# Split weights of the input projection, written to DRAM in the first segment and read back on GpSimd's queue in the second

## The chip, the cores and the metric

The kernel runs on one core of one Trainium2 chip. The metric is the device time of one execution in microseconds (us), the median over runs. The engines are named as in the profile: PE is TensorE (PEld its weight loads), DVE VectorE, ACT ScalarE, POOL GpSimd, SP SyncE, which here only issues transfers.

## The reference

One decoder layer of a hybrid model in f32, with 1024 tokens and 16 learned meta tokens ahead of them, model width 1024:

```
h = concat([meta, x])                                  # 1040 x 1024
h = h + 0.5 * swiglu(rmsnorm(h), ffn1)
u = rmsnorm(h)
aq, ak, av, az, abeta, aalpha, bcols, ga, gb = split(u @ w_in)
o_a = chunked_gated_deltanet(aq, ak, av, az, abeta, aalpha)   # 8 heads of 128
o_b = rwkv7(bcols)                                            # 16 heads of 64
h = h + (sigmoid(ga) * o_a + sigmoid(gb) * o_b) @ w_out
h = h + 0.5 * swiglu(rmsnorm(h), ffn2)
return rmsnorm(h)[:, 16:]
```

The change concerns `u @ w_in`. The result for a token depends on the earlier ones through the recurrences of the two branches, so the tokens are worked off in order.

## The kernel before

**Stages.** `ffn1`, then `middle` (projection, both recurrences, output projection), then `ffn2`. In `middle` the tokens are cut into two segments, of 528 (with the meta tokens) and of 512. Each segment runs through 8 iterations, one for each head of the DeltaNet branch and pair of heads of the RWKV branch; `schedule` (L167) writes out the order of the actions of all 16 iterations (strings at L184 to L189). One iteration projects its columns (`new_b`, `new_a`, `gates`), builds the small triangular systems of 64 and 128 tokens (`operands`), inverts them (`inverses`, `merge_blocks`), forms the transition terms (`transitions`) and runs the chain over the chunks (`chains`, `finish`). The inverses of one iteration are made while the chain of the one before runs. The actions are only written in this order: the scheduler that builds the program decides how the instructions of neighbouring actions are interleaved on each engine.

**The projection.** `w_in` is held as 75 tiles `win` of 128 x 1024 f32 (512 KB), each the weights of 128 columns. f32 products are made of three passes: weights and activations are split into a high part (rounded) and a low part (the rest), and `mm3` (L256) sums high x high, high x low and low x high over 8 blocks of 128 rows, 24 matmuls into one tile `pp` of PSUM. With 528 tokens each is cut in two. Both segments use all 75 tiles, so before the change each is loaded twice and split twice.

**How a tile comes.** `weight_order` (L192) lists all weight tiles in the order of use, `fetchw` (L217) fetches the next one, `loadw` (L229) hands out a tile and first fetches up to `AHEAD` = 1 tiles beyond it. A fetch is a transfer on SP's queue into `wraw` (2 buffers, L223), the high part on ScalarE (L159) and the low part on VectorE (L160), both into `w` (`WB` = 2 buffers of 1 MB). A raw buffer is free when both splits have read it, a split buffer when TensorE has done its matmuls. The weights of the output projection `wout` (L892, tiles `pwo`) take the same way.

**What else stands on these queues.** SP carries nearly all of the program's transfers, in program order per queue. In an iteration these are, beside the raw weights: the operands of the inverse to and from DRAM (`scr`, `scm`, then `Ub`, L1331 to L1342), the inverse's result (`scX`, `scY` written at L1369 and L1371, read as `Xc` at L1374 and as `Y` at L1378), `gp` (L1232), and the small gate weights `ugr` (L1561) and `upr` (L1074). The inverse itself is a chain of 31 pairs of VectorE instructions `tb` and `Xb` (L1364, L1366); its results are merged on TensorE by the tiles `iv` (L1399 to L1423), after GpSimd has copied a part of `Xc` into `XA` (L1380). `ugr` is split into `ug` by the same lines L159 and L160. In `transitions`, VectorE forms `mt` (L1472) and `AR` (L1475) from the tile `mp`, and TensorE forms `np` (L1056) after that. `gra` (L1252) is TensorE's first large product of `operands`, so from `gra` to `iv` TensorE has other work to do until the inverse is there: projection matmuls and the rest of the recurrence.

**The end.** The last two iterations have no new projections behind them. `fill` (L833) makes the output projection of the first segment there, as TensorE's work while the last inverse is made; the other one follows behind.

Of the kernel before, what the change touches and what calls it, by code (L numbers as in the profile page):

```python
# [8 lines left out]
F32 = mybir.dt.float32  # L9
F32R = mybir.dt.float32r  # L10
# [3 lines left out]
P = 128  # L14
D = 1024
KD = D // P
# [23 lines left out]
WB = 2  # L40
AHEAD = 1
S1 = 3
HK = KD // 2
# [63 lines left out]
def build(tc, nc, a):  # L107

    ctx = ExitStack()
    with ctx:  # L110
        g = K()
        g.tc, g.nc, g.a = tc, nc, a
        nc.scalar.preload_act_table_set("natural_log_exp_and_others")
        pad = ctx.enter_context(tc.tile_pool(name="pad", bufs=1, side="right"))
        nc.vector.memset(pad.tile([P, 24], F32, name="pad"), 0.0)
        const = ctx.enter_context(tc.tile_pool(name="const", bufs=1))
        wp = ctx.enter_context(tc.tile_pool(name="wp", bufs=2))
        dram = ctx.enter_context(tc.tile_pool(name="dram", bufs=1, space=bass.MemoryType.DRAM))
        g.mmctx = ctx.enter_context(ExitStack())
        main_banks(g, 2, 3, 8)  # L120
        g.const, g.wp, g.dram = const, wp, dram

        ones = const.tile([P, P], F32, name="ones")
        nc.gpsimd.dma_start(ones, a["ck"][:, :P])
        g.pk = const.tile([P, NPK], F32, name="pk")
        nc.gpsimd.dma_start(g.pk, a["pk"])

        def pv(n):
            o, w = PK[n]
            return g.pk[:, o : o + w]  # L130

        nc.vector.tensor_scalar(pv("omu"), pv("mu"), -1.0, 1.0, op0=ALU.mult, op1=ALU.add)
        nc.vector.tensor_scalar(pv("oka"), pv("ka"), -1.0, 1.0, op0=ALU.mult, op1=ALU.add)
        for n in ("w0", "a0"):
            nc.vector.tensor_scalar(pv(n), pv(n), -1.0, None, op0=ALU.mult)
        g.C = lambda n: ones if n == "ones" else g.ck[:, CK[n][0] - P : CK[n][0] - P + CK[n][1]]
        g.V = lambda n, i=0: g.pk[:, PK[n][0] + i : PK[n][0] + i + 1]

        hdr = [dram.tile([KD, P, sn], F32, name=f"hdr{s}") for s, (_, sn, _) in enumerate(SEGS)]
        mdr = [dram.tile([NJ, P, FULL], F32, name=f"mdr{s}") for s in range(2)]  # L140
        g.hdr, g.mdr = hdr, mdr
        g.sdr = dram.tile([NJ, P, P + CB], F32, name="sdr")
        g.gdr = [dram.tile([NJ, FULL], F32, name=f"gdr{s}") for s in range(2)]
        g.rdr = dram.tile([P, FULL], F32, name="rdr")
        g.h2dr = dram.tile([KD, P, FULL], F32, name="h2dr")
        g.h3dr = dram.tile([KD, P, FULL], F32, name="h3dr")
        g.hid = dram.tile([NF, P, T], F32, name="hid")

        g.worder, g.wready, g.wfetched, g.wused = list(weight_order()), [], 0, 0
        ffn1(g)  # L150
        middle(g)
        ffn2(g)


def split(g, src, hi, lo, eng=None, hi_eng=None):
    if hi_eng:
        hi_eng.tensor_copy(hi, src)
    else:
        g.nc.scalar.activation(hi, src, AF.Copy)  # L159
    (eng or g.nc.vector).tensor_tensor(lo, src, hi.bitcast(F32), op=ALU.subtract)  # L160
# [6 lines left out]
def schedule():  # L167

    last = 2 * NJ - 1
    yield "segment", 0  # L170
    for it in range(2):
        for act in FIRST[it].split():
            yield act, it
    for it in range(last + 1):
        order = {NJ - 2: BEFORE_SWITCH, NJ - 1: SWITCH, last - 1: LAST_BUT_ONE, last: FINAL}.get(it, REGULAR)
        for act in order.split():
            if act == "segment":
                yield act, 1
            else:
                yield act.rstrip("+"), it + act.count("+")  # L180
# [11 lines left out]
def weight_order():  # L192

    def down_order(n):
        f = 0
        for G in GROUPS:
            for _ in range(2 if f + G == NF else 1):
                for m in range(KD):
                    yield f"wdn{n}", (m, slice(None), slice(f, f + G)), G
            f += G  # L200

    def tiles(cts, j=0):
        for ct in cts:
            yield "win", (ct + j % NJ,), KD

    yield from down_order(1)
    for act, it in schedule():
        yield from tiles(USES.get(act, ()), 0 if act == "segment" else it)
    for _ in range(2):
        for m in range(KD):  # L210
            yield "wout", (m,), KD

    yield None
    yield from down_order(2)


def fetchw(g):  # L217
    if not g.worder[g.wfetched]:
        del g.worder[g.wfetched]
    name, idx, kk = g.worder[g.wfetched]  # L220
    g.wfetched += 1
    raw = g.wp.tile([P, KD, P], F32, name="wraw", tag="wraw", bufs=2)
    g.nc.sync.dma_start(raw[:, :kk, :], g.a[name][idx])  # L223
    w = g.wp.tile([P, 2, KD, P], F32R, name="w", tag="w", bufs=WB)
    split(g, raw[:, :kk, :], w[:, 0, :kk, :], w[:, 1, :kk, :])
    g.wready.append((name, idx, w))


def loadw(g, name, *idx):  # L229

    while g.wfetched < min(g.wused + 1 + AHEAD, len(g.worder)) and g.worder[g.wfetched]:
        fetchw(g)
    g.wused += 1
    n, i, w = g.wready.pop(0)
    assert (n, i) == (name, idx)
    return w


def main_banks(g, w, n, banks=6):

    g.mmctx.close()
    g.mmw = w
    pool = lambda name, bufs: g.mmctx.enter_context(
        g.tc.tile_pool(name=name, bufs=bufs, space=bass.MemoryType.PSUM, reuse_waits="tile"))
    g.mm = pool("mm", n)
    g.mx = pool("mx", banks - n * w)
# [19 lines left out]
class Rms:  # L266


    def __init__(self, g, sq, n, add_on=None):
        self.g, self.sq, self.n, self.acc, self.k = g, sq, n, None, 0  # L270
        self.eng = add_on or g.nc.vector
# [276 lines left out]
class Hidden:  # L548

    AHEAD = 3  # L550
# [18 lines left out]
    def ahead(self):  # L569
        for f in range(self.AHEAD):  # L570
            self.load(f)
        yield
        yield
        fetchw(self.g)
        yield
        yield
        self.first = self.put(self.tile(self.pool, F32R, "hd0", "hd0", 1, [2]))
        yield
        yield
# [312 lines left out]
def wout(g, mg, add):  # L892
    for m in range(KD):
        ho = add(m)
        w = loadw(g, "wout", m)
        ps = mm_tile(g, "pwo")
        mm3(g, ps, w, KD, lambda k: (mg[k][:, 0, :FULL], mg[k][:, 1, :FULL]))
        g.nc.vector.tensor_tensor(ho, ps, ho, op=ALU.add)
        yield m, ho
# [796 lines left out]
```

## Time and profile before

| what | value |
|---|---|
| median of three runs | 3086.55 us |
| lowest and highest | 3084.68 and 3089.25 us |
| the profiled execution | 3085.29 us |
| its span in the trace | 3083.5 us |
| TensorE busy | 96% of the span |
| VectorE, ScalarE, GpSimd busy | 64%, 45%, 12% |
| transfers | 287.19 MB, 93 GB/s on average |

How to read it: the profile is one execution, and its span is the time from the first to the last event of the trace; the execution's own time is 1.8 us longer. A row of waits names the waiting engine, the tile and the line, then the engine and the operation that ended the wait, then total us, number and longest. A row of the chain has start and length in us. A row of busy time by stage has the stage, its length, and for each engine the busy time with its count of instructions. In the trace, the first segment's iterations lie from about 800 us to 1474 us, 97 us each; the second segment's steady ones from 1777 us on, 88 us each.

### The profile page before, as it was taken

Reading aid. Unit: us, or ns where it says so; the run is one execution under the profiler, and the core shown is the slowest. Engines: PE = TensorE matmul, PEld = TensorE weight load, DVE = VectorE, ACT = ScalarE, POOL = GpSimd, SP = SyncE. Lnnn points to the kernel's source line nnn. Section 1 sums busy time; section 2 is a strip of 40 time slices with the busy share of each in tenths; the row PEclk is TensorE's granted clock in tenths of the full one; section 3 lists DMA queues with packets and bytes.
Section 4 is the critical chain, followed back from the end, with each engine's and each line's share of the span. In section 5 each row is a group of like instructions: output and inputs, shape, how many; then the busy total and the mean of one; then the engine's idle time right before and its main releaser. Section 6 shows DMA issues by size and latency. Waiting matters only on the chain.

```text
span 3083.5 us, 61656 instructions
## 1 busy us (share of the span) xinstructions
PE 2959.3 (96%) x25498; PEld 2539.0 (82%) x25498; DVE 1976.2 (64%) x3840; ACT 1376.7 (45%) x2404; POOL 354.9 (12%) x519
## 2 busy tenths in 40 slices
PE   8999999999899999999999999999999999999998
PEld 8999998998778888788777777777777888887886
DVE  6455454346677777787867877777866655555335
ACT  5322222126555656566566655665644432222114
POOL 0222220000001000001001000010100022222000
PEclk9999999999899999999999999999999999999999
DMA  3232224234222322333332332223354232224223
GB/s 125 82 97 83 83 86 158 79 101 140 62 74 73 79 70 59 85 79 75 97 89 73 84 81 75 75 75 84 109 148 165 68 104 94 83 83 170 86 78 114
DMA packets 257593, 287.19 MB, mean 93 GB/s; under 512 B 169296, under 2 KB 175440, under 8 KB 257312
## 3 DMA queue, kind: packets, MB, share of 16 engines
q1 hardware_dynamic: 253072, 271.43, 29.4%
q0 software_dynamic: 2512, 8.65, 0.7%
q8 instruction: 201, 3.29, 0.4%
q10 hardware_dynamic: 1728, 3.16, 0.3%
q14 instruction: 80, 0.66, 0.1%
HBM read 232.70 MB, written 50.47 MB: 92 GB/s over the span
## 4 chain that ended last, share of the span: by engine, by line
PE 54%; DVE 11%; ACT 7%; issue 2%; DMA 2%; SPq 0%; DVEq 0%; POOL 0%; ACTq 0%
PE pp L262 18%; PE pg L450 12%; PE pd L262 7%; PE pwo L262 3%; DVE w L160 1%; PE pg L474 1%; PE b L1542 1%; PE cs L1003 1%; PE gra L1252 1%; DMA ugr<-in_upg 1%; PE bkt L1281 1%; DVE tb L1364 1%; DVE mt L1472 1%; DVE Xb L1366 1%; PE vp L1056 1%
## 5 line engine op out<-in xcount | busy, mean ns | idle before, releaser
L262 PE MATMUL pp<-uk,w 128*128 128x512 f32 (+2 forms) x4824 | 975.1, 347 | 15.8 <-DVE w L160 9.3
L262 PEld LDWEIGHTS pp<-uk,w 128*128 128x128 f32 x4824 | 744.7, 191 | 109.1 <-DVE w L160 13.0
L159 ACT ACTIVATE w<-wraw 128x1024 fp32r<-128x1024 f32 (+2 forms) x330 | 326.3, 989 | 712.6 <-PE pd L262 287.6
L262 PE MATMUL pd<-hd,w 128*128 128x512 f32 (+2 forms) x2640 | 495.6, 349 | 11.3 <-DVE w L160 6.7
L262 PEld LDWEIGHTS pd<-hd,w 128*128 128x128 f32 x2640 | 427.5, 189 | 78.2 <-DVE w L160 8.6
L160 DVE TENSOR_TENSOR w<-wraw,w 128x1024 fp32r<-128x1024 f32 (+2 forms) x330 | 376.1, 1140 | 90.9 <-ACT w L159 85.7
L456 DVE TENSOR_TENSOR c<-c,pg 128x520 f32<-128x520 f32 (+1 forms) x280 | 189.2, 689 | 337.3 <-PE pg L450 278.3
L450 PE MATMUL pg<-bt,w 128*128 128x256 f32 (+2 forms) x2520 | 403.9, 317 | 0.0
L450 PEld LDWEIGHTS pg<-bt,w 128*128 128x128 f32 x2520 | 361.0, 188 | 32.9 <-DVE w L160 0.2
L450 PE MATMUL pg<-b,w 128*128 128x256 f32 (+2 forms) x2160 | 348.1, 317 | 0.2 <-DVE c L456 0.2
L450 PEld LDWEIGHTS pg<-b,w 128*128 128x128 f32 x2160 | 309.8, 188 | 28.5 <-PE pg L450 0.4
L419 POOL TENSOR_TENSOR wrx<-wrx 128x512 f32<-128x512 f32 x38 | 57.2, 1505 | 755.1 <-DVE w22b L160 515.3
L1364 DVE TENSOR_TENSOR tb<-Ub,Xb 115x126 f32<-115x126 f32 (+22 forms) x496 | 124.1, 250 | 11.0 <-DMA Ub<-scr 2.7
L1366 DVE TENSOR_TENSOR Xb<-Xb,tb 115x126 f32<-115x126 f32 (+22 forms) x496 | 125.3, 253 | 8.7
L159 ACT ACTIVATE w<-wrx 128x1024 fp32r<-128x1024 f32 (+1 forms) x64 | 58.1, 908 | 156.8 <-PE pg L450 152.3
L1173 DVE SCALAR_TENSOR_TENSOR acc<-xr,pk,acc 128x528 f32<-128x528 f32 (+1 forms) x144 | 109.0, 757 | 26.4 <-ACT acc L1169 25.3
L609 DVE SCALAR_TENSOR_TENSOR h<-pd,h 128x528 f32<-128x528 f32 (+1 forms) x64 | 44.6, 698 | 115.0 <-PE pd L262 115.0
L609 DVE SCALAR_TENSOR_TENSOR hh<-pd,hh 128x512 f32<-128x512 f32 x64 | 44.2, 690 | 109.7 <-PE pd L262 106.6
L262 PE MATMUL pwo<-uk,w 128*128 128x512 f32 x384 | 101.5, 414 | 4.2 <-DVE w L160 1.9
L262 PEld LDWEIGHTS pwo<-uk,w 128*128 128x128 f32 x384 | 73.6, 197 | 22.2 <-DVE w L160 2.7
L923 ACT ACTIVATE sh<-pp,pk 128x528 f32<-128x528 f32 (+1 forms) x54 | 37.5, 694 | 98.3 <-PE pp L262 98.3
L159 ACT ACTIVATE hd<-hr 128x1040 fp32r<-128x1040 f32 (+1 forms) x44 | 45.3, 1061 | 68.6 <-DMA hr<-hid 43.7
(397 smaller groups left out, 4143.1 us busy)
## 6 DMA issues: line engine op xcount, KB each, us to landing
wraw<-in_win SPq DMA_DIRECT2D x150, 512.0 KB
wraw<-in_wgu SPq DMA_DIRECT2D x44, 512.0 KB
wrx<-in_wgu SPq DMA_DIRECT2D x44, 512.0 KB
wraw<-in_wdn SPq DMA_DIRECT2D x48, 320.0 KB
wraw<-in_wdn SPq DMA_DIRECT2D x32, 384.0 KB
hid<-c SPq DMA_DIRECT2D x44, 260.0 KB
hr<-hid SPq DMA_DIRECT2D x22, 520.0 KB
hid<-c SPq DMA_DIRECT2D x44, 256.0 KB
```

The costliest lines, as they stand in the source:

```text
L159: g.nc.scalar.activation(hi, src, AF.Copy)
L160: (eng or g.nc.vector).tensor_tensor(lo, src, hi.bitcast(F32), op=ALU.subtract)
L262: g.nc.tensor.matmul(ps, lhsT=l, rhs=r, start=i == 0, stop=i == n - 1)
L419: sums.tensor_tensor(a22, a21, a22, op=ALU.add)
L450: nc.tensor.matmul(ps[:, c0 : c0 + cn], lhsT=l[:, x, k, :], rhs=r[:, k, y, c0 : c0 + cn], start=i == 0, stop=i == 3 * HK - 1)
L456: nc.vector.tensor_tensor(o, x, y, op=ALU.add)
L474: nc.tensor.matmul(ps[:, c0 : c0 + cn], lhsT=l[:, x, k, :], rhs=r[:, k, y, c0 : c0 + cn], start=i == 0, stop=i == 6 * HK - 1)
L609: nc.vector.scalar_tensor_tensor(hv, pd, 0.5, hv, op0=ALU.mult, op1=ALU.add)
L923: nc.scalar.activation(sh[:, 1 : 1 + n], ps, AF.Identity, scale=g.V("mu", i))
L1173: nc.vector.scalar_tensor_tensor(acc[:, :n], xr[:, tap : tap + n], V("convw", ct * 4 + tap), acc[:, :n], op0=ALU.mult, op1=ALU.add)
L1364: nc.vector.tensor_tensor(tv, U[:, i, i + 1 :].unsqueeze(2).to_broadcast([npt, nt, ncc]), X[:, i, 0:ncc].unsqueeze(1).to_broadcast([npt, n ...
L1366: nc.vector.tensor_tensor(X[:, i + 1 :, 0:ncc], X[:, i + 1 :, 0:ncc], tv, op=ALU.add)
```

## The change

In the first segment, each split tile of `win` is also written to DRAM as it is (both parts, 1 MB) by SP's queue. In the second segment `fetchw` loads no raw tile of `win` and splits none: `saved_tile` reads the split one back on GpSimd's queue. Two of three tiles come into a buffer of `w`; every third comes as two halves of 512 KB (k-blocks 0 to 3 and 4 to 7), into both buffers of `wraw`, and the class `Halves` hands `mm3` the block of the right half. So three tiles can be held at once, and `loadw` fetches one tile further ahead in the second segment. The output projection's tiles still come raw, through `wraw`.

```
@@ before ffn1(g)
+        g.wsp = dram.tile([75, P, 2, KD, P], F32, name="wsp")
+        g.wsaved = {}
+        g.wsecond = next(i for i, x in enumerate(g.worder) if x and x in g.worder[:i] and x[0] == "win")
@@ fetchw
-    raw = g.wp.tile([P, KD, P], F32, name="wraw", tag="wraw", bufs=2)
-    g.nc.sync.dma_start(raw[:, :kk, :], g.a[name][idx])
-    w = g.wp.tile([P, 2, KD, P], F32R, name="w", tag="w", bufs=WB)
-    split(g, raw[:, :kk, :], w[:, 0, :kk, :], w[:, 1, :kk, :])
+    if name == "win" and idx[0] in g.wsaved:
+        w = saved_tile(g, idx[0])
+    else:
+        raw = g.wp.tile([P, KD, P], F32, name="wraw", tag="wraw", bufs=2)
+        g.nc.sync.dma_start(raw[:, :kk, :], g.a[name][idx])
+        w = g.wp.tile([P, 2, KD, P], F32R, name="w", tag="w", bufs=WB)
+        split(g, raw[:, :kk, :], w[:, 0, :kk, :], w[:, 1, :kk, :])
+        if name == "win":
+            g.nc.sync.dma_start(g.wsp[idx[0]], w.bitcast(F32))
+            g.wsaved[idx[0]] = len(g.wsaved)
     g.wready.append((name, idx, w))
+class Halves:
+    def __init__(self, *ts):
+        self.ts = ts
+    def __getitem__(self, i):
+        p, x, k, m = i
+        return self.ts[k // HK][p, x, k % HK, m]
+def saved_tile(g, ct):
+    if g.wsaved[ct] % 3 < 2:
+        w = g.wp.tile([P, 2, KD, P], F32R, name="w", tag="w", bufs=WB)
+        g.nc.gpsimd.dma_start(w, g.wsp[ct].bitcast(F32R))
+        return w
+    ts = []
+    for k in range(2):
+        t = g.wp.tile([P, 2, HK, P], F32R, name="wh", tag="wraw", bufs=2)
+        g.nc.gpsimd.dma_start(t, g.wsp[ct][:, :, k * HK : (k + 1) * HK, :].bitcast(F32R))
+        ts.append(t)
+    return Halves(*ts)
 def loadw(g, name, *idx):
-    while g.wfetched < min(g.wused + 1 + AHEAD, len(g.worder)) and g.worder[g.wfetched]:
+    ahead = AHEAD + (name == "win" and idx[0] in g.wsaved and g.wused >= g.wsecond)
+    while g.wfetched < min(g.wused + 1 + ahead, len(g.worder)) and g.worder[g.wfetched]:
         fetchw(g)
```

In the program VectorE and ScalarE have 75 instructions fewer, GpSimd has 100 more (50 tiles `w`, 25 tiles of two halves `wh`), and SP as many as before (75 stores for 75 raw loads). Since the scheduler sets the order anew, other instructions move too. Lines of the kernel after stand 36 higher from `mm3` on.

VectorE in the first segment, an iteration's start before (`mt` and `AR` are the transition terms, `ug` and `upz` the small gate weights, `LT` the operands of the next inverse):

```order
L160 TENSOR_TENSOR w<-wraw,w 128x1024
L160 TENSOR_TENSOR ug<-ugr,ug 128x128
L1566 TENSOR_TENSOR ug<-ugr,ug 32x128
L1078 TENSOR_TENSOR upz<-upr,upz 64x128 x2
L1472 TENSOR_TENSOR mt<-mp,ck 64x4x64 x4
L1475 TENSOR_TENSOR AR<-mp,AR 128x4x64 x2
L1214 TENSOR_TENSOR LT<-grb,ck 128x4x128 x2
```

and after:

```order
L1508 TENSOR_TENSOR mt<-mp,ck 64x4x64 x2
L1511 TENSOR_TENSOR AR<-mp,AR 128x4x64
L1514 TENSOR_TENSOR vbk<-np,vbk 128x4x64
L1517 TENSOR_TENSOR yb<-np,yb 128x4x64
L1276 TENSOR_TENSOR kts<-gp,tk 128x4
L1514 TENSOR_TENSOR vbk<-np,vbk 128x4x64
L1517 TENSOR_TENSOR yb<-np,yb 128x4x64
L1515 TENSOR_TENSOR vbk<-vbk,gam 128x512
L1250 TENSOR_TENSOR LT<-grb,ck 128x4x128 x2
L1536 COPY rhm<-bm_14575 16x128
L164 TENSOR_TENSOR ug<-ugr,ug 128x128
L1602 TENSOR_TENSOR ug<-ugr,ug 32x128
```

The splits of `ug` stood directly ahead of `mt` and `AR`; now they stand behind them, and behind the sums with `np`.

SP in the first segment, from the inverse's result to the gate weights, before:

```order
L1369 DMA scX<-Xb 1536x1x16 x2
L1371 DMA scY<-Yt 816x1x32 x2
L1374 DMA Xc<-scX 128x12x32
L223 DMA wraw<-in_win 128x1024
L1378 DMA Y_7138<-scY 32x12x32 x4
L1384 DMA ym<-scY 16x2x16
L1385 DMA ym<-scY 16x16
L223 DMA wraw<-in_win 128x1024 x2
L1232 DMA gp<-gdr_88 128x512
L223 DMA wraw<-in_win 128x1024 x2
L1561 DMA ugr<-in_upg 128x256
```

and after:

```order
L1410 DMA Xc<-scX 128x12x32
L234 DMA wsp<-w 128x2048
L1414 DMA Y_7141<-scY 32x12x32 x4
L1420 DMA ym<-scY 16x2x16
L1421 DMA ym<-scY 16x16
L230 DMA wraw<-in_win 128x1024 x2
L234 DMA wsp<-w 128x2048
L230 DMA wraw<-in_win 128x1024
L234 DMA wsp<-w 128x2048
L230 DMA wraw<-in_win 128x1024
L234 DMA wsp<-w 128x2048
L1268 DMA gp<-gdr_88 128x512
```

A store `wsp` of 1 MB now stands between `Xc` and `Y`, where a raw load stood, and three more ahead of `gp`.

TensorE in the last iteration, before (`pp` is the projection, `gat` the gate, `pwo` the output projection, `iv` the first merge of the last inverse):

```order
L262 MATMUL pp<-uk,w 128x512 x11
L1003 MATMUL cs<-hl,bdr 128x512
L262 MATMUL pp<-uk,w 128x512 x7
L1003 MATMUL cs<-hl,bdr 128x512
L262 MATMUL pp<-uk,w 128x512 x43
L1581 MATMUL gat<-gds,ug 128x512 x3
L1581 MATMUL gat<-g_17736,ug 128x512
L262 MATMUL pwo<-uk,w 128x512 x85
L1399 MATMUL iv_26390<-Xc,LT 32x32 x16
L1399 MATMUL iv_26390<-Xc,UA 32x32 x8
```

and after:

```order
L298 MATMUL pp<-uk,w 128x512 x29
L298 MATMUL pp<-uk,wh 128x512 x24
L1617 MATMUL gat<-gds,ug 128x512 x3
L1617 MATMUL gat<-g_17804,ug 128x512
L1435 MATMUL iv_26296<-Xc,LT 32x32 x16
L1435 MATMUL iv_26296<-Xc,UA 32x32 x8
L298 MATMUL pwo<-uk,w 128x512
```

The 85 matmuls of the output projection that stood ahead of `iv` now stand behind it.

## The prediction

> **What bounds the kernel now.** I read the page first, then busy time by stage, then the waits of TensorE, then the chain of two iterations, and last the rows of the operations that the change touches. The page:
>
> ```profile
> span 3083.5 us, 61656 instructions
> PE 2959.3 (96%) x25498; PEld 2539.0 (82%) x25498; DVE 1976.2 (64%) x3840; ACT 1376.7 (45%) x2404; POOL 354.9 (12%) x519
> wraw<-in_win SPq DMA_DIRECT2D x150, 512.0 KB
> ```
>
> TensorE is busy for 2959.3 of 3083.5 us, and the change leaves its work alone (the same matmuls in another order). So what can be won is a part of 3083.5 - 2959.3 = 124.2 us of idle time, over the whole program; the splits and loads that go matter only where TensorE waits. By stage, the second column of numbers is the length, the third TensorE's busy time, and the last two the DMA share and GB/s: six iterations of the first segment, the switch between the segments, five iterations of the second segment, and the end of the recurrences:
>
> ```profile
> 893.00:1474.00 581.00, 554.31 (x6792) 474.86 (x6794) 440.42 (x1072) 341.13 (x697) 47.52 (x139) 1.00 0.28 74
> 1474.00:1777.00 303.00, 282.82 (x2962) 222.88 (x2964) 236.76 (x545) 181.94 (x345) 26.02 (x53) 0.98 0.32 85
> 1777.00:2216.00 439.00, 423.44 (x4625) 338.08 (x4621) 349.61 (x815) 263.59 (x501) 38.23 (x80) 1.00 0.30 80
> 2216.00:2400.00 184.00, 175.52 (x1473) 137.43 (x1470) 117.55 (x239) 79.22 (x142) 1.46 (x3) 0.97 0.49 157
> ```
>
> TensorE idles 581.00 - 554.31 = 26.7 us, then 20.2, 15.6 and 8.5 us. These four numbers bound what each stage can give back. What TensorE waited for in the first segment (first row), at the switch (next two) and in the steady second segment (last three), with total, times and longest:
>
> ```profile
> PE np L1056 <- DVE AR L1475: 6.4, 6, 2.3
> PE pp L262 <- DVE gg L1582: 3.4, 1, 3.4
> PE pp L262 <- DVE w L160: 3.4, 2, 2.8
> PE np L1056 <- DVE AR L1475: 4.7, 5, 2.0
> PE xp L1056 <- ACT at L1460: 2.7, 5, 1.0
> PE pp L262 <- DVE w L160: 0.6, 2, 0.4
> ```
>
> The wait for split weights itself is small: 0.6 us in five iterations of the second segment. A gain there comes mainly from VectorE and ScalarE being less busy when the recurrence needs them.
>
> **Part 1: the splits that go.** The rows of the raw tiles from the switch to the end:
>
> ```profile
> L159 ACT ACTIVATE w<-wraw x79: 1040/1052/1084, 1487.9 to 2258.7; 128x1024 fp32r<-128x1024 f32 x79
> L160 DVE TENSOR_TENSOR w<-wraw,w x79: 1206/1218/1310, 1489.0 to 2260.1; 128x1024 fp32r<-128x1024 f32 x79
> ```
>
> and VectorE's group in the five steady iterations alone:
>
> ```profile
> L160 DVE TENSOR_TENSOR w<-wraw,w 128x1024 fp32r<-128x1024 f32 x45 | 55.1, 1225 | 5.7 <-ACT w L159 5.6
> ```
>
> 75 of these 79 go (the others are the output projection's): 75 x 1.052 = 78.9 us of ScalarE and 75 x 1.218 = 91.4 us of VectorE. Nearly all of it lies beside TensorE's work. In the steady second segment the upper bound is the whole idle time, 15.6 us. I take 9: the 4.7 us of the np row (its chain through VectorE keeps the `ug` split ahead of it, but loses projection splits), the 2.7 us of the xp row in part and the 0.6, and about 2 us of shorter waits. Lower bound: the new loads wait behind other work on GpSimd and cost 8 us (third rival). At the switch the upper bound is 20.2 us; the two waits shown, 3.4 and 3.4 us, are on VectorE, which is busy for 236.76 of 303.00 us there and has some 25 splits less (the 79 without the 45 of the steady stretch and the handful of the end). I take 9, with bounds of 0 and 20.2.
>
> **Part 2: the read back.** Each tile is now 1 MB, where the raw one had 512 KB. The nearest loads on GpSimd's queue are 520 KB:
>
> ```profile
> L670 POOL DMA_DIRECT2D h<-in_hT x8: 527/530/557, 477.6 to 486.6; - x8
> DMA to landing us min/median/max: 5.1/8.5/15.1
> ```
>
> A 1 MB load should then take between 5.1 us (if the time is latency) and 2 x 8.5 = 17 us (if it is all transfer). I take about 9, near the median row, since eight loads shared the queue there. By the Trainium skill, "DMA: Bandwidth & Descriptors", section "Measured (HBM→SBUF, 128 partitions, SWDGE, issued from GpSimd)", a lone 1 MB load takes 6.15 us; by that the loads would be early with more to spare and the sum would not move. In TensorE's order a tile is asked for when the tile three before it is done, so two tiles of projection lie between. One matmul of 512 columns takes 9.77 / 43 = 0.227 us (row in part 4), a tile 24 x 0.227 = 5.5 us, two tiles 10.9 us: more than 9, less than 17. Recurrence work between them adds cover, so I cost this at nothing; without that cover 75 tiles could each show some of the 6 us. Each issue takes 0.53 us of GpSimd, 100 x 0.53 = 53 us of an engine that was busy 12%.
>
> A rule that speaks against the move: the waits of SP's queue,
>
> ```profile
> SPq L223 <- DVE w L160: 743.7, 156, 24.0
> ```
>
> are long (743.7 us over 156 waits), and moving loads off SP shortens what is queued behind them. The Trainium skill, the same page, section "Issuing engines are not separate DMA queues", says that all issuing engines share the same 16 DMA engines and that issuing from several saves only sequencer time. By that rule alone the move is worth nothing and costs the second half of each read; with DMA shares of 0.28 to 0.32 in the rows above there is room for it, and I keep the sum.
>
> **Part 3: the stores in the first segment.** 75 stores of 1 MB go on SP's queue, each ready when its split is. The chain of one iteration there, in order of time:
>
> ```profile
> 1181.05 3.47 DMA ugr<-in_upg
> 1187.83 0.43 DVE AR L1475
> 1188.40 1.33 PE np L1056 x56
> 1193.80 1.73 PE gra L1252 x8
> 1260.29 0.96 PE iv L1399 x48
> ```
>
> and SP's part that carries the inverse back:
>
> ```profile
> 1240.29 1.41 SPq L1369 DMA_DIRECT2D scX<-Xb  x2
> 1245.74 3.09 SPq L1374 DMA_DIRECT2D Xc<-scX  x1
> 1248.94 1.01 SPq L223 DMA_DIRECT2D wraw<-in_win  x1
> 1250.95 1.92 SPq L1378 DMA_DIRECT2D Y<-scY  x4
> ```
>
> Two things change. First, before, `AR` stood on VectorE behind the split of `ug`, whose raw tile landed late (3.47 us on the chain); after, the order puts `AR` ahead of it. The gain is at most the 6.4 us of the np row in the six iterations. I take 4. Second, between gra and iv the order had 315 projection matmuls in each of these iterations; after, it has 247 and 289 by turns. At 0.227 us per 512 columns (the tile of 528 columns is cut in two) that is 39.8 us before, and 35.0 and 39.2 after. Y's last issue ended at 1250.95 + 1.92 = 1252.87 and iv began at 1260.29, so landing and slack are 7.4 us together. After, cover is down by 4.8 us in every other iteration, and a 1 MB store stands directly ahead of Y on SP. Part 2 prices 1 MB at 9 us as a load; no store of that size is in the trace. If Y waits for none of it, the 4.8 us eat into the 7.4 and cost nothing; if Y waits for all of it, 4.8 + 9 - 7.4 = 6.4 us show in three of the six, and 9 - 7.4 = 1.6 in the others, 24 us in all. I take 2.3 us in each of three, 7 in all, nearer to nothing because stores and small transfers can run side by side at a DMA share of 0.28. Part 3 is -4 + 7 = +3 us, bounds -6.4 and +24.
>
> **Part 4: the end.** The last iteration's chain:
>
> ```profile
> 2225.43 1.92 PE gra L1252 x8
> 2253.84 9.77 PE pp L262 x43
> 2264.54 5.96 PE pwo L262 x26
> 2270.51 13.67 PE pwo L262 x59
> 2284.18 0.96 PE iv L1399 x48
> 2281.04 2.03 SPq L1378 DMA_DIRECT2D Y<-scY  x4
> ```
>
> Before, 26 + 59 = 85 matmuls of the output projection (19.6 us) covered the wait for the last inverse, and iv began just as Y was there (its last issue ended at 2283.07, iv began at 2284.18). After, the last projection tile comes as two halves in both raw slots, so the output projection's raw tiles can only be loaded when it is used up: order puts iv ahead of all of `pwo`, and 24 + 29 projection matmuls ahead. Counted between gra and iv, 179 projection matmuls become 112: 67 x 0.227 = 15.2 us less cover. VectorE's inverse loses four to seven splits of 1.218 us in that stretch (4.9 to 8.5 us), so TensorE would stand for 15.2 - 8.5 = 6.7 to 15.2 - 4.9 = 10.3 us. A part of it replaces the 8.5 us of idle time that were there. I take +7, with bounds +2 and +14.
>
> **Sum.** +3 - 9 - 9 + 7 = -8 us. The profiled execution took 3085.29 us (span 3083.5 and 1.8 around it), 1.3 under the median of the three runs, 3086.55; 3086.55 - 8 gives 3078.5. A change of 0.2%, 6 us, is about what a measurement of this kernel can tell from none. The lower bounds together (-6.4 - 20.2 - 15.6 + 2 = -40) and the upper ones (+24 + 0 + 8 + 14 = +46) are unlikely to meet.
>
> **Rivals.**
> - *Slower: the stores delay the recurrence.* Place: Y, `Ub` and `ugr` behind 1 MB stores on SP in the first segment. Price: the 24 us of part 3, plus some 4 for the seventh iteration of the segment; with the second segment's -18 and the end's +7 that is +17, or 3103.6. It decides from where a store delays Y by more than the 7.4 us less the 4.8. Against it: DMA share 0.28. For it: the small load of `ugr` already puts 3.47 us on the chain there. Chance 0.18.
> - *No change: the work that goes was beside TensorE.* The wait for split weights was 0.6 us in five iterations, so steady state and switch give some 10 together, and part 3 and 4 take them: 3086.5, within 6 us. Chance 0.22.
> - *Slower: GpSimd's queue is in order.* A tile's load stands behind the copy of XA, which waits for Xc. In the second segment that holds back the tile that follows iv. At 3 us in each of six iterations 18 us replace the steady gain of 9: 3086.5 + 3 - 9 + 18 + 7 = 3105.5, and 3096.5 where half of it shows. It decides where Xc lands later than the 10.9 us of two tiles ahead of the use. Chance 0.08.
> - *Slower: GpSimd's descriptor writes meet VectorE.* Each of the 100 issues would take longer beside VectorE's two-input work; the row above has 527 to 557 ns for eight issues, 30 ns apart, while VectorE worked. If each of 75 tiles came 0.3 us late, 22 us are lost: 3078.5 + 22 = 3100.5. Beside this stands the Trainium skill, "DMA: Bandwidth & Descriptors", section "SWDGE vs HWDGE vs iDMA", which says that these rings are written in SBUF under the lock that VectorE can hold. Chance 0.04.
> - *Much faster.* All of the idle time of switch and steady second segment goes (-20.2 - 15.6), and the rest stands at +3 + 7: -25.8, 3060.7. Chance 0.14.
> - That the change doesn't do what it says is ruled out by the order's counts: VectorE and ScalarE lose 75 rows each, GpSimd gains 100.
>
> **How the numbers follow.** The forecast of 3078.5 has 0.34; a tenth of that falls within 6 us of no change. Faster by over 0.2%: 0.31 + 0.14 = 0.45. Within: 0.22 + 0.03 = 0.25. Slower: 0.18 + 0.08 + 0.04 = 0.30. The range leaves out the ends: from 3058, somewhat under the much faster case, to 3105, where the slower cases end. The forecast's own range is 3066 to 3086. Both signs hold much of the chance.
>
> **What would show it.** In the profile after, by the same stages: no idle time of TensorE behind AR in the first segment, and the store's landing near 9 us; iv directly behind Y there would be the first rival. The switch and the five steady iterations should idle 9 us less each; a wait of `pp` for a DMA of `w` or `wh` is the third rival. At the end TensorE should stand some 7 us ahead of iv. Wrong I would be if the first segment is longer by over 10 us, or if the steady iterations keep their 15.6 us of idle time.

## The result, and the profile after

The changed kernel takes 3141.7 us (median of 4 runs, 3137.47 to 3145.62), the kernel before beside it 3087.9 us: a ratio of 1.0169 with a 95% interval of 1.0154 to 1.0184. It is slower by 1.7%, some 54 us, where 3078.5 was forecast with a range of 3058 to 3105. The page after:

```profile
span 3138.0 us, 61716 instructions
PE 3001.5 (96%) x25498; PEld 2578.4 (82%) x25498; DVE 1902.0 (61%) x3765; ACT 1314.6 (42%) x2329; POOL 392.8 (13%) x619
wsp<-w SPq DMA_DIRECT2D x75, 1024.0 KB
w<-wsp POOLq DMA_DIRECT2D x50, 1024.0 KB, 5.3
```

TensorE does the same 25498 matmuls, and is busy for 3001.5 us instead of 2959.3: 42 of the 54 us show as busy time. The splits are gone as counted (75 instructions fewer, their row on VectorE 376.1 to 284.0 us, VectorE as a whole 1976.2 to 1902.0). To see where the time lies I cut both programs at the same event, the first `np` of an iteration: five iterations of the first segment, the switch, six steady iterations of the second, and the rest. Busy time by stage before:

```profile
992.40:1477.60 485.20, 463.52 (x5629) 396.22 (x5630) 368.73 (x895) 282.59 (x574) 37.38 (x115) 1.00 0.29 76
1477.60:1700.30 222.70, 207.03 (x2129) 163.02 (x2130) 170.22 (x388) 131.24 (x246) 19.77 (x40) 0.98 0.31 82
1700.30:2223.00 522.70, 502.11 (x5548) 400.57 (x5549) 418.04 (x975) 317.28 (x605) 44.48 (x93) 1.00 0.31 83
2223.00:3083.50 860.50, 834.22 (x4220) 678.79 (x4220) 468.45 (x693) 273.88 (x390) 121.46 (x99) 0.99 0.33 108
```

and after:

```profile
999.90:1520.30 520.40, 486.65 (x5602) 418.76 (x5603) 372.41 (x896) 281.57 (x574) 29.80 (x115) 0.93 0.50 158
1520.30:1752.30 232.00, 215.10 (x2127) 170.02 (x2127) 151.12 (x370) 119.29 (x237) 34.58 (x65) 0.96 0.53 151
1752.30:2263.70 511.40, 500.67 (x5589) 399.32 (x5589) 363.26 (x926) 270.67 (x548) 78.78 (x166) 1.00 0.51 138
2263.70:3138.00 874.30, 842.29 (x4238) 685.65 (x4238) 467.47 (x692) 274.57 (x391) 122.21 (x102) 0.98 0.33 109
```

Length by stage: +7.5 us up to the first cut (992.4 to 999.9), then +35.2, +9.3, -11.3 and +13.8, together the 54.5 us by which the span grew. In the five iterations TensorE's busy time rose by 23.1 us and its idle time by 12.1, with the granted clock at 0.93 instead of 1.00. The third row holds the gain that was looked for: idle time fell from 20.6 to 10.7 us.

The first segment, in windows of 4 us around one `iv` after (behind the window and its length stands TensorE's busy time; the third number from the right is its granted clock):

```profile
1272.00:1276.00 4.00, 2.41 (x60) 2.09 (x58) 4.00 (x9) 2.74 (x5) 1.97 (x8) 1.00 1.07 325
1276.00:1280.00 4.00, 2.95 (x53) 2.01 (x54) 3.42 (x7) 0.97 (x2) 0.00 (x0) 0.62 0.48 113
1280.00:1284.00 4.00, 1.98 (x28) 1.69 (x22) 1.25 (x4) 2.49 (x5) 0.00 (x0) 0.50 0.43 174
1284.00:1288.00 4.00, 4.00 (x74) 3.67 (x73) 2.72 (x4) 2.33 (x5) 0.00 (x0) 0.60 0.01 4
```

and what TensorE did there, with the idle time ahead and its releaser in brackets:

```profile
1273.56 0.75 PE L1435 MATMUL iv<-Xc,LT 32*32 32x32 f32 x32 [0.17 <-DMA Xc<-scX]
1277.05 0.80 PE L1039 MATMUL bon<-hl,bdr 128*128 128x512 f32 x1 [2.46 <-ACT hl L163]
1282.02 1.08 PE L1454 MATMUL iv<-XA,UA 64*64 64x64 f32 x8 [1.55 <-DVE XA L1450]
1288.20 11.89 PE L298 MATMUL pp<-uk,w 128*128 128x272 f32 x96
```

`iv` began as soon as `Xc` was there. Between its stages stood no projection matmul, so TensorE waited for a column sum (`bon`) and for `XA`, and from the end of the first of these two gaps on the clock stood at half for some 10 us. Only then came 96 projection matmuls in one piece. The waits of the five iterations:

```profile
PE cs L1039 <- ACT hl L1053: 8.1, 5, 3.7
PE bon L1039 <- ACT hl L163: 7.8, 5, 2.5
PE np L1092 <- DVE AR L1511: 7.0, 5, 2.7
PE iv L1454 <- DVE XA L1450: 4.6, 3, 1.6
```

The chain before has the next `gra` 30 us behind `iv` (1260.29, and the row below); after, 46 us:

```profile
1290.50 1.73 PE gra L1252 x8
```

```profile
1214.62 1.73 PE gra L1288 x8
1273.56 1.05 PE iv L1435 x48
...
1319.48 1.73 PE gra L1288 x8
```

From `gra` to `iv` it is 58.9 us after instead of 66.5, so the inverse is ready sooner for the recurrence, and what was gained there is lost behind it.

That is the order of every other iteration. In those between, 289 projection matmuls stand ahead of `iv`, 48 between its stages and 10 from there to `np` (before: 315, 30 and 8), and they take as long: 104.4 us from `gra` to `gra` around the `iv` at 1383.61, against 104.9 in the one shown. Here TensorE waited for the column sums `cs` with nothing ahead of them, and the 48 came behind; before, 16 projection matmuls stood at that place. After, then before:

```profile
1390.85 0.81 PE L1039 MATMUL cs<-hl,onesr 128*128 128x256 f32 x2 [3.67 <-ACT hl L1053]
1394.12 6.31 PE L298 MATMUL pp<-uk,w 128*128 128x272 f32 x28
```

```profile
1264.66 3.93 PE L262 MATMUL pp<-uk,w 128*128 128x512 f32 x16
```

In both kinds of iteration the stretch from `gra` to `iv` is shorter than before, and the one from `iv` to the next `gra` is 8 to 16 us longer.

### The profile page after: what moved, and what is told of

Its sections match the earlier page's. It is cut to its first block, busy times and chain, and to the rows that moved or that the text cites. A ratio compares the mean times of both kernels' runs of the same rounds, so it can differ in the third digit from the quotient of the medians.

```text
span 3138.0 us, 61716 instructions
## 1 busy us (share of the span) xinstructions
PE 3001.5 (96%) x25498; PEld 2578.4 (82%) x25498; DVE 1902.0 (61%) x3765; ACT 1314.6 (42%) x2329; POOL 392.8 (13%) x619
## 4 chain that ended last, share of the span: by engine, by line
PE 81%; DVE 7%; ACT 5%; DMA 4%; issue 2%; SPq 1%; POOL 0%; DVEq 0%; ACTq 0%; POOLq 0%
PE pg L486 25%; PE pp L298 20%; PE pd L298 15%; PE pg L510 3%; PE pwo L298 3%; PE cs L1039 1%; PE xp L1092 1%; PE b L1578 1%; PE vp L1092 1%; PE gra L1288 1%; DMA Xc<-scX 1%; PE grb L1247 1%; PE bkt L1317 1%; PE mp L1092 1%; PE np L1092 1%
## 5 line engine op out<-in xcount | busy, mean ns | idle before, releaser
L298 PE MATMUL pp<-uk,w 128*128 128x512 f32 (+2 forms) x4224 | 823.3, 342 | 7.9 <-DMA w<-wsp 4.5
L298 PEld LDWEIGHTS pp<-uk,w 128*128 128x128 f32 x4224 | 641.7, 194 | 76.1 <-issue 11.3
L163 ACT ACTIVATE w<-wraw 128x1024 fp32r<-128x1024 f32 (+2 forms) x255 | 247.3, 970 | 694.7 <-PE pd L298 290.7
L298 PE MATMUL pd<-hd,w 128*128 128x512 f32 (+2 forms) x2640 | 496.3, 350 | 10.6 <-DVE w L164 6.5
L164 DVE TENSOR_TENSOR w<-wraw,w 128x1024 fp32r<-128x1024 f32 (+2 forms) x255 | 284.0, 1114 | 96.8 <-ACT w L163 92.3
L298 PE MATMUL pp<-uk,wh 128*128 128x512 f32 x600 | 161.1, 403 | 0.0
L298 PEld LDWEIGHTS pp<-uk,wh 128*128 128x128 f32 x600 | 109.0, 189 | 19.6
```

The costliest lines, as they stand in the source:

```text
L298: g.nc.tensor.matmul(ps, lhsT=l, rhs=r, start=i == 0, stop=i == n - 1)
```

## The experiments

Two theories stood against each other. **Theory A (order):** a store on SP's queue makes the scheduler place projection matmuls behind the inverse instead of beside it; TensorE runs dry around `iv`, its clock falls, and the iteration grows. **Theory B (traffic):** 75 MB of stores put off the transfers on the recurrence's path. Times below are medians, ratios against the kernel before beside them.

**e1, small stores on SP.**

```
-            g.nc.sync.dma_start(g.wsp[idx[0]], w.bitcast(F32))
+            g.nc.sync.dma_start(g.wsp[idx[0]][0:8], w[0:8].bitcast(F32))
...
```

> Edit: the change, but of each split tile only 8 of 128 partitions are stored (64 KB instead of 1 MB), and the read back takes 1 MB of the raw weights instead (the output is of other numbers). The order of the instructions on TensorE, VectorE and ScalarE is that of the change to the row. Theory A (order: the store on SP's queue makes the scheduler lay the projection matmuls elsewhere, TensorE runs dry around iv and np, and its granted clock drops there): the first segment stays as long as with the change, about 104 us an iteration, and the whole stays at 3135 to 3145 us. Theory B (traffic: 75 MB of stores delay the transfers of the inverse): nearly all of the 43 us of the first segment come back, 3095 to 3105 us.

3134.2 us, ratio 1.0142 (1.0127 to 1.0157). Without 15/16 of the bytes only 7.5 us came back. The five iterations still take 514.9 us at a clock of 0.95:

```profile
999.20:1514.10 514.90, 480.35 (x5603) 412.53 (x5604) 372.42 (x896) 281.00 (x574) 31.57 (x115) 0.95 0.30 75
```

Theory B alone falls for this order, and theory A came out as it said. The DMA share is back at 0.30, so the clock does not follow the traffic. The small store is still in the program here; what that leaves open is taken up with e9.

**e2, full stores on GpSimd's queue.**

```
-            g.nc.sync.dma_start(g.wsp[idx[0]], w.bitcast(F32))
+            g.nc.gpsimd.dma_start(g.wsp[idx[0]], w.bitcast(F32))
```

> Edit: the change with the stores issued on GpSimd's queue instead of SP's. All 75 MB are still stored; TensorE's order in the first segment is that of the kernel before (315 projection matmuls from gra to iv in each iteration). Theory A (order): the first segment goes back to 97 us an iteration within 1 us, the whole to 3095 to 3105 us. Theory B (traffic): the first segment stays at 102 us an iteration or more, the whole at 3130 to 3145 us.

3151.8 us, ratio 1.0195 (1.0176 to 1.0214): TensorE's order of before, and slower than the change. Theory A alone falls here. The chain over the length of an iteration has transfers on it:

```profile
1187.67 4.32 DMA wraw<-in_win
1217.14 8.29 DMA upr<-in_upwa
1240.04 7.47 DMA Ub<-scr
```

Before, the piece of that kind on the chain was `ugr` with 3.47 us, and no `Ub`. In the five iterations ScalarE waited longest for the raw tile that it splits:

```profile
ACT w L163 <- DMA wraw<-in_win: 28.8, 5, 6.0
```

**e3, the read back alone.**

```
-            g.nc.sync.dma_start(g.wsp[idx[0]], w.bitcast(F32))
-        g.nc.gpsimd.dma_start(w, g.wsp[ct].bitcast(F32R))
+        g.nc.gpsimd.dma_start(w, g.a["win"][min(ct, 73) : min(ct, 73) + 2].rearrange("t p k m -> p t k m").bitcast(F32R))
...
```

> Edit: no stores; in the second segment 1 MB of raw weights is read on GpSimd's queue for each tile as if it were the split one (the output is of other numbers). TensorE's order in the first segment is that of the kernel before. Both theories: the first segment as before, 97 us an iteration; steady second segment 86.5 us an iteration as with the change; the end longer by 14 us as with the change. Whole: 3085 to 3100 us. If the first segment is still slow here, both theories fall.

3092.7 us, ratio 1.0014 (1.0004 to 1.0023). The first segment has the order of before and in this trace ends 4.6 us later (1482.2 against 1477.6); the steady second segment gains as much as with the change, 511.1 us where before had 522.7:

```profile
1709.60:2220.70 511.10, 500.77 (x5589) 399.34 (x5590) 363.24 (x926) 270.63 (x548) 88.56 (x166) 1.00 0.52 138
```

But switch and end are longer by 4.7 (227.4 against 222.7) and 9.7 us (870.2 against 860.5), and the whole gains nothing.

**e4, the stores alone.**

```
-    if name == "win" and idx[0] in g.wsaved:
+    if False:
-    ahead = AHEAD + (name == "win" and idx[0] in g.wsaved and g.wused >= g.wsecond)
+    ahead = AHEAD
-        if name == "win":
+        if name == "win" and idx[0] not in g.wsaved:
```

> Edit: the stores alone; in the second segment the raw weights are loaded and split as before, nothing is read back. Both theories: the first segment as with the change (104 us an iteration, +43 us), the second and the end as before: 3125 to 3140 us. By theory A it equals the change in the first segment, since the order there is the same.

3140.6 us, ratio 1.0164 (1.0149 to 1.0179): the stores cost what the whole change costs.

**e5, small stores on GpSimd's queue.**

```
-            g.nc.gpsimd.dma_start(g.wsp[idx[0]], w.bitcast(F32))
+            g.nc.gpsimd.dma_start(g.wsp[idx[0]][0:8], w[0:8].bitcast(F32))
...
```

> Edit: the stores on GpSimd's queue (as in the run before with 1 MB each, 3151.8 us), but only 8 of 128 partitions of each tile (64 KB), and the read back takes raw weights (the output is of other numbers). The order on TensorE, VectorE and ScalarE is that run's to the row. Theory B (traffic): with TensorE's order of before, the 1 MB stores put off the landing of Ub and of the gate weights by 3 to 5 us each, 6 to 10 us an iteration; without the bytes the whole goes to 3092 to 3102 us. Theory C (GpSimd's queue: a store that waits for its split holds back the copies and memsets behind it): the whole stays above 3135 us.

3094.9 us, ratio 1.0022 (1.0012 to 1.0032). With the order of e2 to the row and without its bytes, 57 us are gone, so in this order the bytes cost them, and neither GpSimd's queue nor 75 waiting issues on it cost anything to speak of. ScalarE's wait for raw tiles is 2.7 us here. Which of the late transfers, raw tiles, `upr` or `Ub`, costs how much no run isolates. The landing of `Ub` in five iterations, first in e2:

```profile
DMA to landing us min/median/max: 7.3/7.4/7.5
```

then in e5:

```profile
DMA to landing us min/median/max: 4.1/4.4/4.6
```

**e6, the store issued when the tile is handed out.**

```
     g.wused += 1
     n, i, w = g.wready.pop(0)
+    if n == "win" and i[0] not in g.wsaved:
+        g.nc.sync.dma_start(g.wsp[i[0]], w.bitcast(F32))
+        g.wsaved[i[0]] = len(g.wsaved)
...
```

> Edit: the change with each store issued on SP's queue when the tile is handed out to TensorE, not when it is fetched. All 75 MB are stored. TensorE's order has 277 projection matmuls from gra to iv in the first segment and 66 between the merges of the inverse, where the change has 247 or 289, and 48 or 0. Theory A (order: TensorE runs dry around iv): most of the 30 us that the small stores still cost go, what is left is the traffic: 3105 to 3120 us. Theory B (traffic costs 6 to 10 us an iteration wherever the order leaves no slack): 3135 to 3150 us.

3124.3 us, ratio 1.0119 (1.0103 to 1.0135), between the two expectations: the place of a store in the program is worth 17 us, with the same bytes.

**e7, the last projection tile whole (on e3).**

```
-    if g.wsaved[ct] % 3 < 2:
+    if g.wsaved[ct] % 3 < 2 or ct == g.wlast:
...
```

> Edit: the read back alone (no stores, raw weights read; the output is of other numbers), and the last projection tile comes whole into a buffer of w, so that the raw buffers are free for the output projection. TensorE has 143 matmuls ahead of the last iv instead of 112 (31 x 0.227 = 7 us). Theory of the end (the halves in the raw buffers push the output projection behind the last inverse): 4 to 7 us under the read back alone at 3092.7, 3086 to 3089 us. Rival (the output projection is only moved, TensorE's wait there is not from it): within 2 us of 3092.7.

3090.8 us, ratio 1.0004 (0.9994 to 1.0014). That is 2 us under e3, at the rival's edge, and the intervals overlap so far that 4 us, the least that the theory expected, can't be ruled out: 7 us more of work ahead of `iv` gave some 2.

**e8, no further lookahead (on e3).**

```
-    ahead = AHEAD + (name == "win" and idx[0] in g.wsaved and g.wused >= g.wsecond)
+    ahead = AHEAD
```

> Edit: the read back alone (no stores, raw weights read; the output is of other numbers) without the further tile of lookahead. TensorE's order is the same as with it. If two tiles of lead cover the landing of 1 MB, as the prediction has it, one tile (5.5 us of matmuls and what stands between) does so only in part: 5 to 20 us slower than 3092.7. If the loads are early anyway: within 2 us of it.

3094.4 us, ratio 1.0020 (1.0011 to 1.0030): within 2 us. TensorE's order is the same with and without it, and the loads are early with either; in the steady second segment of the change the 1 MB loads land in

```profile
DMA to landing us min/median/max: 5.1/5.3/7.2
```

**e9, e6 with small stores.**

```
-        g.nc.sync.dma_start(g.wsp[i[0]], w.bitcast(F32))
+        g.nc.sync.dma_start(g.wsp[i[0]][0:8], w[0:8].bitcast(F32))
...
```

> Edit: as the run with each store issued when its tile is handed out (3124.3 us), on SP's queue, but only 8 of 128 partitions (64 KB), with the read back from raw weights (the output is of other numbers). TensorE's, VectorE's and ScalarE's order is that run's to the row. Theory A+B (two costs: the order of the fetch-time store leaves TensorE without work around iv, and the bytes delay the transfers of the recurrence): with this order and no bytes both are gone, 3090 to 3100 us. Rival D (a store on SP's queue, however small, holds back what is queued behind it until its split is there): above 3115 us.

3121.1 us, ratio 1.0113 (1.0098 to 1.0129): the bytes are some 3 us of e6's 35, within the intervals, and the two theories together had expected 3090 to 3100. That spoke for rival D as much as for the order, since both runs with small stores on SP were long (e1, e9) and the one on GpSimd's queue was not (e5), and their orders differ too. SP's rows speak against D. In e1, `scX` is issued directly behind the last `Xb`, and `Y` 10.6 us after `scX`, as in the kernel before (1240.29 to 1250.95):

```profile
1257.74 1.61 SPq L1405 DMA_DIRECT2D scX<-Xb  x2
...
1266.30 1.02 SPq L234 DMA_DIRECT2D wsp<-w  x1
1268.37 1.86 SPq L1414 DMA_DIRECT2D Y<-scY  x4
```

And ahead of `scr`, the inverse's operands, the queue stood ready and waited for VectorE's `LT` in e1's five iterations for nearly as long as before (before, then e1):

```profile
SPq L1331 <- DVE LT L1214: 55.2, 5, 12.0
SPq L1367 <- DVE LT L1250: 52.5, 5, 11.2
```

So in e1 the stores hold back neither the operands of the inverse nor, in the iteration shown, its result.

**e13 and e14, the order alone, without any store.** The kernel before, with a part of `new_a` written behind `merge_blocks` in iterations 1 to 7 (e13 its third projection tile, e14 its second and third), its matmuls held until the last of `iv` is issued:

```
+EARLY = "merge_blocks new_v+ transitions operands+ inverses+ chains gates finish new_b++ new_a++"
...
+def new_v(g, q):
+    tiles_a(g, q, ((2, 16),), g.lastiv)
...
+    with ExitStack() as after:
+        if behind is not None:
+            after.enter_context(g.tc.issue_after(behind.ins))
```

> Edit: the kernel before, no stores, no read back; in the first segment the third projection tile of new_a (iterations 1 to 7) is written behind merge_blocks, and its matmuls are held until the last iv matmul is issued. From gra to iv TensorE has 288 projection matmuls instead of 315, none between the iv stages, and 56 instead of 38 from iv to np. Theory A (what lengthens the first segment is projection work that stands behind the inverse instead of beside it): 27 matmuls of half a tile's width at 0.126 us are 3.4 us an iteration, 6 to 7 iterations, and some loss at the halved clock: 3105 to 3125 us. Rival D (the store on SP's queue itself, whatever TensorE's order): within 4 us of before, 3084 to 3093 us.

> Edit: as the run before, with the second and the third tile of new_a held: 238 projection matmuls from gra to iv, 115 from iv to np (the change has 247 and 58, or 289 and 111, by turns). Theory A: 77 x 0.126 = 9.7 us an iteration, 3135 to 3165 us. Rival D: within 4 us of before.

3158.1 us, ratio 1.0225 (1.0212 to 1.0239), and 3169.3 us, ratio 1.0270 (1.0255 to 1.0285). With no store in the program, the order alone costs 71 and 82 us (VectorE's and ScalarE's work on the moved tiles moves with them), so rival D isn't needed. The change's own order without any store was not run, so how much of e1's 45 us is the order's alone is not measured. The size is not what theory A said (3105 to 3125 for e13): 27 matmuls moved cost as much as 77 nearly, so a price for each matmul is wrong. In e13's five iterations the clock is 0.94 and the long wait is the one that was seen in the change:

```profile
1017.30:1546.80 529.50, 482.20 (x5632) 411.90 (x5632) 366.91 (x896) 283.98 (x575) 33.63 (x115) 0.94 0.26 69
```

```profile
PE cs L1008 <- ACT hl L1022: 23.6, 5, 4.7
```

A column sum that waits up to 4.7 us stands among the stages of `iv`, with no projection ahead of it to hide that: the picture of the change's iterations with 289 matmuls ahead of `iv`, where it waits 3.67. In e14 the waits are of another kind, `iv` for `Xc` (11.6 us), `Y` (9.9) and `XA` (12.2): there too little is left beside the inverse, as in the change's iterations with 247, whose waits for `XA` are 4.6 us in three.

```profile
PE iv L1437 <- DVE XA L1433: 12.2, 5, 2.4
```

**e10, one small load early (on e7).**

```
+    sl = slice(64, 72)
+    rs = tmp_tile(g, "rsA")[sl, :n]
+    nc.sync.dma_start(rs, g.a["ck"][sl, NSB + 16 - off : NSB + 16 - off + n])
     wa = shifted(g, c, 56, 24, "wa")
...
```

The reason for it is the wait at the switch in e3, and its chain:

```profile
PE tkp L1014 <- DVE c L1000: 9.6, 1, 9.6
```

```profile
1548.41 13.38 DMA scY<-Yt
...
1564.75 4.85 DMA rsA<-in_ck
1569.69 1.23 DVE c L1000
```

A load of 8 rows, `rsA`, stood on SP's queue behind `Y`, which waited for `scY`; TensorE, with fewer splits to wait for, came there early and stood.

> Edit: the read back alone with the last projection tile whole (3090.8 us; the output is of other numbers), and the small constant rsA loaded at the start of its block, so that on SP's queue it stands ahead of the inverse's transfers, not behind Y. TensorE's order is the same. Theory: at the switch TensorE's 9.6 us wait for tkp is for this load, which stood behind Y and so behind scY's landing; without it the read back shows its gain, 3078 to 3084 us. Rival (the wait is for other work on VectorE): within 3 us of 3090.8.

3086.7 us, ratio 0.9997 (0.9988 to 1.0006): 4 us under e7, where 7 to 13 were expected. The wait for `tkp` fell to 1.4 us, and the next small load behind `Y` took its place:

```profile
PE pw L1120 <- ACT upz L1113: 7.8, 1, 7.8
```

**e15, both small loads early.**

```
+    if s:
+        g.up8 = load_up(g, 0)
...
+    raw = g.up8 if it == NJ else load_up(g, j)
```

> Edit: the read back alone (no stores; the output is of other numbers) with the last projection tile whole and rsA loaded early (3086.7 us), and the first small weights upr of the second segment loaded at that block's start too, ahead of the inverse's transfers on SP's queue. At the switch TensorE waited 7.8 us for upz, which is made of upr. Theory (small loads behind Y hold the switch): 3077 to 3083 us, clear of the kernel before. Rival (the switch is bound by VectorE and ScalarE, and the next wait takes over): within 3 us of 3086.7.

3077.7 us, ratio 0.9962 (0.9950 to 0.9974): the read back alone now gains 10 us by the medians (the profiled execution, 3080.1 us, is one of the longer ones). The switch takes 218.1 us where before had 222.7:

```profile
1476.80:1694.90 218.10, 207.08 (x2068) 162.84 (x2068) 147.35 (x363) 114.87 (x227) 32.76 (x64) 0.98 0.48 131
```

**e12 and e16, the same loads early in the kernel before.** The edits of e10, and of e10 and e15, in the kernel before.

> Edit: the kernel before with rsA loaded early, nothing else. There TensorE did not wait for tkp at the switch, so nothing should change: within 3 us of before (3089). A gain of over 5 us would say that the switch's wait was the same in the kernel before.

> Edit: the kernel before with both small loads (rsA and the first upr of the second segment) early, no stores, no read back. If the 10 us under before of the last run of the read back (3077.7 us) are the read back's, this stays within 4 us of before (3084 to 3092 us). If they are the small loads' alone, this reaches 3077 to 3082 us, and would beat both kernels without any of the change.

3091.8 us, ratio 1.0009 (1.0000 to 1.0018), 3.9 us over the kernel before beside it, and 3088.4 us, ratio 1.0002 (0.9993 to 1.0011). Neither gains. The gain of e15 is the read back's, which the two small loads had hidden.

**e11, the whole change at its best:** e6's place of the store, e7's last tile and e10's load.

> Edit: the whole change with the store issued when the tile is handed out, the last projection tile whole, and rsA loaded early; it computes what the reference does. Sum of the parts: 3124.3 - 2 - 9 = 3113 us (3108 to 3118). It does not come under the kernel before by either theory, since 75 MB of stores are still there.

3123.9 us, ratio 1.0114 (1.0098 to 1.0130): nothing under e6, 11 us over the expected sum of the parts and 6 over the sum with the 4 us that e10 measured. No run that stores the tiles whole comes near the kernel before; the read back is worth 10 us at most in these runs, and the whole stores cost 30 or more (e6 against e3: 3124.3 - 3092.7). So no version here that computes what the reference does beats both kernels. Storing only some of the tiles was not tried.

## Why the prediction was wrong

- **Steady second segment, -9.** Right: -11.3 us in six iterations where five were counted, which is -9.4 for five; idle time 20.6 to 10.7 us.
- **The read back, 0.** Right in the steady part. The 1 MB load landed in 5.1 to 7.2 us where 9 was taken, within about 1 us of the 6.15 that the Trainium skill gives for a lone one ("DMA: Bandwidth & Descriptors", section "Measured (HBM→SBUF, 128 partitions, SWDGE, issued from GpSimd)"); its figure is the time that the DMA engines are busy, ours runs from issue to landing. Taking the lookahead away changed nothing that shows (e8). The GpSimd rivals did not come: issues of whole tiles took 541 to 588 ns, of halves 703 to 837, and e5 shows no cost of the queue.
- **The switch, -9.** Wrong: +9.3. The step took VectorE's busy time for the bound and gave back its share. The switch hangs on small loads queued behind the inverse's transfers on SP. With them out of the way it gains (e15: -4.6), about half of what was forecast. After, 4.5 us of the loss is a wait of `pp` for a 1 MB load at the start of the read back, the sign that the prediction gave for its third rival; but no copy of `XA` stands ahead of it. It was issued at 1570.29, 2 us behind the last store, and landed some 10 us later. In e1 and e3, which read raw weights there and have no whole stores, `pp` has no such wait; no run isolates it.
- **The first segment, +3, bounds -6.4 and +24.** Wrong, and it decides: +42.7 (7.5 and 35.2). The step that failed is this one: the 68 and 26 projection matmuls that left the stretch from `gra` to `iv` were booked as less cover for a wait ahead of `iv`, at 7 us in all. That wait did not come: `gra` to `iv` got shorter. The work did not vanish but went behind `iv`, into the stretch that the next inverse waits for, where TensorE also stood for `bon`, `cs` and `XA` with nothing to fill in. The prediction read the order up to `iv` and not what stood among its stages: by turns no matmul where there were 30, or 48 of which none stood ahead of the column sums. In the second kind its cover fell by only 0.6 us (39.8 to 39.2), and the iteration is as long as the other. And it had no term for the clock: around `iv` it fell to half, and 23.1 of the 35.2 us are TensorE's own busy time. How the loss divides between the waits and the clock that they brought down was not isolated.
- **The 4 us of np.** Not there: 7.0 us in five iterations instead of 6.4 in six. `AR` lost the `ug` split ahead of it on VectorE, but still came late.
- **The first rival** had the right sign and the right segment, and a mechanism that is real but not the one that decides here. In the order of before the stores' bytes cost 57 us (e2 against e5), by later raw tiles, `upr` and `Ub`; in the change's order 7.5 (e1). The change's order costs 45 with hardly any bytes (e1), another order 71 with none (e13). The two don't add; that a late transfer finds slack where the order already makes the recurrence wait is a likely reading that was not tested.
- **The end, +7, bounds +2 and +14.** +13.8, at the edge. The mechanism is doubtful: TensorE stood for `Xc` ahead of `iv` for 3.0 us, not 7 to 10, and with 7 us more of output projection there some 2 came back (e7). That the total came within the bounds is in part luck. Part of it is again the clock (0.98 against 0.99 over the last 860 us, some 8 us of busy time). The rest is open.

## What to carry to other kernels

When a scheduler sets the order, read what it put behind the late result as carefully as what it put ahead: work that leaves the cover of a wait is paid where it goes, and a dry spot among short dependent matmuls can be paid again at half clock, as here. A transfer that only runs beside the work can still cost through its place in a queue: it changes the order, and it delays small transfers that the recurrence waits for, so try it with a fraction of its bytes and on another queue before trusting either. When a stage is freed of work and doesn't get faster, look for the small load that stands in a queue behind something slow.

## What the runs showed of the hardware

The granted clock fell to 0.50 after gaps that were far from a full stop. In the iteration shown it was still 0.98 of full in the microsecond from 1276 to 1277 and 0.50 in the next one, at the end of the gap of 2.46 us; it stayed at half through the gap of 1.55 us and through work without a gap, until some 10 us after its fall. In the iteration after that one it fell with less idle time:

```profile
1384.00:1388.00 4.00, 2.33 (x94) 1.96 (x86) 0.80 (x2) 3.23 (x7) 1.10 (x6) 0.77 0.67 228
```

In windows of 1 us it was 1.00 from 1385 to 1386 and 0.59 in the next one; the gaps just ahead were of 0.59 and 0.26 us, among the `iv` matmuls of 32x32, and the wait of 3.67 us came when the clock was down already. The Trainium skill, "TensorE: Matmul & The Clock Gate", section "Part 1: The HAM clock gate (the "warmup" mystery)", tells of the drop after an idle window of about 3.4 us; here no gap ahead of either fall was that long. What brings it down, the gaps or the small matmuls, no run isolates.

With 1 MB stores on GpSimd's queue (e2, 161 GB/s) the landing of the 192 KB `Ub` took 7.4 us, where stores of 64 KB (e5) left it at 4.4, though the DMA share in e2 was only 0.51.
